# The first up pairs of an encoder layer: product 3 in a bank of its own, the order of their products, and the order of w_o's transposes

## The chip, the core and the metric

The kernel runs on one core of a Trainium2 chip, as one program. The time is that of the device in microseconds (us), the median of several executions. The engines are TensorE (PE, with PEld for its loads of weights, which run beside the matmuls), VectorE (DVE), ScalarE (ACT), GpSimd (POOL) and SyncE (SP). Each has its own instruction stream and works it off in order; they meet at semaphores. DMAs are issued by SP and POOL here. PSUM has eight banks of 128 partitions x 512 fp32 numbers; matmuls write there, and ScalarE and VectorE read from there.

## The reference

One layer of a streaming encoder on 512 tokens, in float32, cut to what matters (D_MODEL 2048, D_FF 5632, eight heads of 128):

```
h  = rms_norm(x, pre_mix_g)
z  = h @ w_in                        # [q | k | v | u]
m  = concat(chunked_attention(q, k, v, rel_bias),
            multiscale_pool(u, pool_w, pool_scale)) @ w_o
x  = x + rms_norm(m, post_mix_g)
h  = rms_norm(x, pre_ffn_g)
up = causal_dwconv(h @ w_up, conv_w, conv_b)      # 3 taps along the tokens
y  = (gelu(up[..., :D_FF]) * up[..., D_FF:]) @ w_down
x  = x + rms_norm(y, post_ffn_g)
```

The change lies where `h @ w_o` ends and `h @ w_up`, the convolution and the gate begin.

## The kernel before

**Numbers.** A float32 operand is split into a rounded part and the rest: `split(hi, lo, src)` is one ScalarE copy that rounds (line 140) and one VectorE subtraction (line 141). Names that end in h are rounded parts, names that end in l are rests. A product of two split operands needs three matmuls (`mm3`: hi by hi, hi by lo, lo by hi; lines 162 to 165).

**Seven products.** The large matrix products are made in blocks of two by two with seven block products instead of eight, numbered 1 to 7. For w_up this holds from the third *pair* on; a pair is 256 columns of w_up, and there are 44 pairs. The first two are *plain* (made with `mm3` into banks `up`, L162 to L165). The other 42 are counted by k from 0, and (k,i) is product i of pair k. Each such product multiplies a factor of h, which is made once, by a factor of w_up, which is made for each product, in `mm2`: eight matmuls of 128x512 (the rounded part of the weights, L170) and eight of 128x256 (the rests, L176). Products 6, 7 and 4 are *turned*: their narrow matmuls come first.

A product adds into a bank of PSUM, named q and a letter and k: products 1, 6, 7, 4 of a pair add up in bank a (qa_k), 5 and 3 in bank g (qg_k), and 2 has bank d (qd_k). Products 1, 5 and 2 begin a bank (`FIRST`); the others add onto what is there. As a bank also holds sums that are wanted in between, the function `keep(k, i)`, called right after the matmuls of (k,i), reads them out: after 1, one half is copied by ScalarE and the other added by VectorE to `first_parts`; after 2, VectorE adds both halves of qd there; after 5, ScalarE copies qg (L1413); after 6, ScalarE copies qa (L1418), and VectorE adds qg, which by then holds 5 and 3 (L1419); after 7, ScalarE copies qa (L1422), and VectorE adds the copy of 5; after 4, `keep_all(k)` puts the pair's four quarters together. So the next product that adds onto a bank must wait for the ScalarE copy of what stands there.

**Taps, gate, product.** A finished pair is convolved (`taps`: one ScalarE step L1309, two VectorE steps L1310 and L1311). Two pairs belong together: the first of them goes through gelu (`gate`, L1332), the second is multiplied by it on VectorE (`product`, L1342) in two halves, and the result goes to memory in two stores that POOL issues (L1345). The scratch tiles are four holders, m8, zc, x01 and x23, cut into parts: m8 holds the copy of 5, the sums of 6 and 7, and the value half before its multiplication, zc the finished pair and the gate.

**Weights' factors.** `Factors` makes the factor of each product, in the order of a list `order`. `load` issues the raw blocks on SP (wx or x, wy, wz). `make` splits a raw block into a tile pair (wfh, wfl) and, after products 1, 5, 6 and 3, has POOL add another block of w_up onto the same raw tile with an accumulating DMA (`add`, L1109): the block that is x for product 1 becomes the factor of 5, then 6, then 4, and y that of 3, then 7. Such a DMA must wait for the split before it, on ScalarE and VectorE, and the next split for the DMA. `get` is called ahead of each product: it counts the use and has the factors of up to AHEAD = 4 products made in advance (and up to 3 before `open` is set), and the raw loads run RAW - AHEAD = 6 further ahead. There are eight tiles for split weights (the ring w4), so four pairs hi and lo.

**What sets the order.** TensorE's instructions run in the order in which the program writes them. Those of all the other engines are put into an order by the compiler's scheduler, and where a ring or a pool hands out a tile, the writer waits for its last reader.

The list `order` begins with products 1 and 2 of the pairs 0 to 3, which run while the second half of h (tokens 256 to 511) is still being normalized, and among which `turn_back` transposes that half; then come the two plain pairs (the entries "w"), then (0,5), (0,3), and then all other products sorted by 7 k + place_of[i]. During the first plain pair `h_sums` makes the factors h5, h6 and h3 of h (tiles h50, h51, h60, h61, h30, h31). In that part gT0 to gT3 are the tiles of split h, made by the split at the end of `turn_back` (L141 with the output gT), and w00_0 to w00_3 and w10_0 to w10_3 the four weights of each plain pair.

`turn_back(0, pair, ...)` does the same for tokens 0 to 255, in eight steps of two blocks, called by `first_half(q)` behind the four pieces of the w_o product before (two steps for each piece). The steps 0 to 3 go to the tile a11, 4 to 7 to a12, and after each odd one a quarter is split.

Of the kernel before, what the change touches and what calls it, by code (L numbers as in the profile page):

```python
# [81 lines left out]
def encoder_layer(ctx: ExitStack, tc: tile.TileContext, x, xT, vecs, rel, post_mix, post_ffn,  # L82
# [7 lines left out]
    nc = tc.nc  # L90
# [15 lines left out]
    def bank(name):  # L106
        return psum.tile([P, 512], F32, tag="ps", name=name)
# [246 lines left out]
    hT = new_gT()  # L354
# [5 lines left out]
    for kb in range(KD):  # L360
        i, o = divmod(kb, 8)
# [9 lines left out]
        for what in "qk":  # L371
            _, hi, lo = first[f"{what}0_{i}"]
# [160 lines left out]
    BANK = {1: "a", 6: "a", 7: "a", 4: "a", 5: "g", 3: "g", 2: "d"}  # L533
    FIRST = 1, 5, 2
# [367 lines left out]
    if True:  # L902
# [104 lines left out]
        def turn_back(t0, pair, ps):  # L1007

            for k in range(2):
                kb = 2 * pair + k  # L1010
                for t in range(2):
                    nc.tensor.transpose(ps[:, k * T + t * P:k * T + (t + 1) * P],
                                        hn[t0 + t][:, kb * P:(kb + 1) * P], ident)
            v = wholes[pair // 4, t0 // 2]
            for k in range(2):
                kb = 2 * pair + k
                nc.scalar.activation(v[:, kb % 8, :], ps[:, k * T:(k + 1) * T], AF.Copy, scale=col(V_PREFFN, kb))
            if pair % 2:
                i = pair // 2 % 2
                split(*quarter(pair // 4, t0 // 2, i), v[:, 4 * i:4 * i + 4, :])  # L1020
# [8 lines left out]
        for t in range(2):  # L1029
            load_x(t, acc8(f"x{t}", "B"))  # L1030
        hT = new_gT()
        hT[1], hT[2] = hT[2], hT[1]
        x2(0, y11, 0, whole)
        x2(0, y12, 1, whole)
        keep_x(0)
# [21 lines left out]

        def first_half(q):
            for i in range(2):
                turn_back(0, 2 * q + i, wo_banks[4 + (2 * q + i) % 4])  # L1060

        finish_last(0, wo_product(4, 0, a22, first_half))
        load_x(3, h8(0, "x3"))
# [1 line left out]
        class Factors:  # L1065
# [3 lines left out]
            def __init__(self):  # L1069
                n = 2 * NU - PLAIN  # L1070

                self.alone, self.open = (1, 2, 3, n - 1), False
                place_of = {1: 0, 6: 8, 2: 2, 7: 10, 5: 4, 4: 12, 3: 6}
                begin = [(k, i) for k in range(4) for i in (1, 2)] + [(0, 5), (0, 3)]
                end = [(n - 1, 5), (n - 2, 6), (n - 1, 3), (n - 1, 1), (n - 2, 7), (n - 1, 6), (n - 2, 4),
                       (n - 1, 7), (n - 1, 2), (n - 1, 4)]
                order = sorted((7 * k + at, k, i) for k in range(n) for i, at in place_of.items())
                self.order = begin + [(k, i) for _, k, i in order if (k, i) not in begin + end] + end  # L1080
                self.order[8:8] = [("w", q) for q in range(4 * PLAIN)]
                self.raw, self.made, self.loaded, self.used = {}, [], 0, 0
# [58 lines left out]
            def get(self):  # L1141
                self.used += 1
                self.prefetch(0)
                self.prefetch(self.AHEAD if self.open else self.AHEAD - 1)
                v, self.made[self.used - 1] = self.made[self.used - 1], None
                return v

# [157 lines left out]
    if True:  # L1305
# [55 lines left out]
        def h_factor(i, kb):  # L1361
            if i in hs:
                return hs[i][kb // 4][:, kb % 4].rearrange("p a b -> p (a b)"), 0
            k, t = {1: (0, 0), 7: (0, 1), 2: (1, 0), 4: (1, 1)}[i]
            return hT[2 * k + kb // 4][:, kb % 4, 2 * t:2 * t + 2].rearrange("p a b -> p (a b)"), 1 - t
# [35 lines left out]
        def keep(k, i):  # L1401

            if i == 1:
                v = zs[k, "1"] = first_parts[:, k % 4, :]
                nc.scalar.activation(v, banks[k, "a"][:, :T], AF.Copy)
                nc.vector.tensor_add(v, banks[k, "a"][:, T:], v)
            elif i == 2:
                v, d = zs[k, "1"], banks.pop((k, "d"))
                nc.vector.tensor_add(v, d[:, :T], v)
                nc.vector.tensor_add(v, d[:, T:], v)  # L1410
            elif i == 5:
                zs[k, "5"] = raw_x("zb")[:, :S] if k == end else holder("m8")[1]
                nc.scalar.activation(zs[k, "5"], banks[k, "g"], AF.Copy)  # L1413
            elif i == 6:
                m = raw_x("zm") if k == end else holder("m8")[2]
                zs[k, "m"] = m.rearrange("p (a b c) -> p a b c", a=2, b=2)
                v = wide(zs[k, "m"][:, :1])
                nc.scalar.activation(v, banks[k, "a"], AF.Copy)  # L1418
                nc.vector.tensor_add(v, banks.pop((k, "g")), v)  # L1419
            elif i == 7:  # L1420
                v = wide(zs[k, "m"][:, 1:])
                nc.scalar.activation(v, banks[k, "a"], AF.Copy)  # L1422
                nc.vector.tensor_add(v, zs.pop((k, "5")), v)
            elif i == 4:
                keep_all(k)

# [12 lines left out]

        def seven(k, i):  # L1440
            w = factors.get()
            if i in FIRST:
                banks[k, BANK[i]] = bank(f"q{BANK[i]}_{k}")
            ps = banks[k, BANK[i]]
            mm2(ps, w, [h_factor(i, kb) for kb in range(8)], i in FIRST, i in TURNED)

        def first_left():

# [323 lines left out]
```

## Time and profile before

| what | us |
|---|---|
| median of three runs | 1864.54 (1862.0 to 1865.09) |
| the profiled execution's own time | 1864.22 |
| its span in the profile | 1862.4 |
| TensorE without work, start to 50 | 1.44 |
| 560 to 580, the first plain up pair begins | 1.58 |
| 620 to 700, the first of the 42 pairs | 5.10 |
| 1350 to 1440, the down projection begins | 2.59 |
| 1800 to the end | 8.2 |

The mean granted clock of TensorE over the span is 0.997 of full speed. The products (k,i) run from 620 to about 1370 us.

How the views are read: a timeline's row gives the start, the duration, the engine, the line of the program, the operation and its output and inputs (the buffers' numbers left out); a bracket at its end gives the time that the engine stood idle before the row and what ended it, with the line of the instruction that did. The table of waits has the waiting engine, output and line, the releaser behind the arrow, and then the sum in us, the number, and the longest. In the table by windows each engine has its busy time and, in parentheses, its count of instructions.

### The profile page before, as it was taken

The numbers are of one execution on the slowest core, as the hardware profiler recorded it, in microseconds if no ns is written. First come the engines' busy times: TensorE is split into PE (matmuls) and PEld (weight loads), VectorE is DVE, ScalarE is ACT, GpSimd is POOL, SyncE is SP. The second block draws the span as 40 slices with busy tenths as digits, with TensorE's granted clock in tenths as the row PEclk, the third lists the DMA queues.
The fourth block names the chain that finished last, engine by engine and source line by source line (L and its number), as shares of the span: only waits on it lengthen the run. The fifth ranks groups of instructions, "written<-read, shape, count | busy, mean of one in ns | idle before, by whom it ended". The sixth has DMA issues, their size and how long they took to land.

```text
span 1862.4 us, 25317 instructions
## 1 busy us (share of the span) xinstructions
PE 1843.5 (99%) x9514; PEld 1580.2 (85%) x9514; DVE 1482.2 (80%) x1772; ACT 1101.1 (59%) x1442; POOL 306.9 (16%) x407
## 2 busy tenths in 40 slices
PE   9999999999999999999999999999999999999998
PEld 7888888888888788888888888888888888888886
DVE  6988778888678677777787777877776899899876
ACT  7655455456586566665666656666555665565553
POOL 3412001100001212212122122221221001111101
PEclk9999999999999999999999999999999999999999
DMA  8599977999879888988988888888888977777785
GB/s 317 175 318 301 323 226 232 269 278 321 324 270 291 184 187 206 201 206 199 206 199 207 206 196 204 198 209 205 200 174 278 356 226 173 194 207 179 176 243 145
DMA packets 139546, 428.63 MB, mean 230 GB/s; under 512 B 12000, under 2 KB 15456, under 8 KB 133728
## 3 DMA queue, kind: packets, MB, share of 16 engines
q0 software_dynamic: 55440, 175.66, 47.0%
q1 hardware_dynamic: 83984, 251.36, 38.1%
q8 instruction: 75, 1.23, 0.3%
q14 instruction: 47, 0.39, 0.1%
HBM read 372.97 MB, written 104.33 MB: 256 GB/s over the span
## 4 chain that ended last, share of the span: by engine, by line
PE 66%; DMA 1%; DVE 1%; ACT 1%; issue 0%; POOL 0%; DVEq 0%; POOLq 0%; ACTq 0%
PE qa L170 16%; PE qa L176 8%; PE qg L170 8%; PE qg L176 4%; PE pa L165 4%; PE pa L162 4%; PE pa L164 4%; PE qd L170 4%; PE pg L165 2%; PE pg L162 2%; PE pg L164 2%; PE qd L176 2%; PE pd L164 1%; PE pd L165 1%; PE pd L162 1%; PE up L164 1%
## 5 line engine op out<-in xcount | busy, mean ns | idle before, releaser
L170 PE MATMUL qa<-gT,wfh 128*128 128x512 f32 x1176 | 295.9, 394 | 0.0
L141 DVE TENSOR_TENSOR wfl<-x,wfh 128x1024 fp32r<-128x1024 f32 x161 | 197.1, 1224 | 83.0 <-ACT wfh L140 76.8
L170 PEld LDWEIGHTS qa<-gT,wfh 128*128 128x128 f32 x1176 | 212.5, 190 | 38.2
L140 ACT ACTIVATE wfh<-x 128x1024 fp32r<-128x1024 f32 x161 | 170.1, 1056 | 88.9 <-PE qg L170 47.3
L1109 POOL DMA_DIRECT2D x<-in_w_up x122 | 104.7, 858 | 475.1 <-DVE wfl L141 435.7
L176 PE MATMUL qa<-gT,wfl 128*128 128x256 f32 x1176 | 165.1, 283 | 3.4 <-ACT m L1418 3.4
L170 PE MATMUL qg<-h,wfh 128*128 128x512 f32 x672 | 166.4, 390 | 1.9 <-ACT m L1413 1.9
L176 PEld LDWEIGHTS qa<-gT,wfl 128*128 128x128 f32 x1176 | 155.0, 192 | 8.8 <-ACT m L1418 4.7
L170 PEld LDWEIGHTS qg<-h,wfh 128*128 128x128 f32 x672 | 125.8, 188 | 28.9 <-ACT m L1413 2.9
L140 ACT ACTIVATE wfh<-wy 128x1024 fp32r<-128x1024 f32 x98 | 103.3, 1054 | 69.1 <-PE qd L170 49.3
L141 DVE TENSOR_TENSOR bl<-b,bh 128x2048 fp32r<-128x2048 f32 x56 | 127.1, 2286 | 18.6 <-ACT bh L140 11.7
L140 ACT ACTIVATE bh<-b 128x2048 fp32r<-128x2048 f32 x56 | 106.0, 1913 | 54.7 <-DVE b L1229 22.7
L141 DVE TENSOR_TENSOR wfl<-wy,wfh 128x1024 fp32r<-128x1024 f32 x98 | 119.4, 1218 | 16.9 <-ACT wfh L140 14.6
L162 PE MATMUL pa<-bh,ah 128*128 128x512 f32 x320 | 124.5, 389 | 0.0
L164 PE MATMUL pa<-bl,ah 128*128 128x512 f32 x320 | 124.5, 389 | 0.0
L165 PE MATMUL pa<-bh,al 128*128 128x512 f32 x320 | 124.5, 389 | 0.0
L176 PEld LDWEIGHTS qg<-h,wfl 128*128 128x128 f32 x672 | 91.7, 190 | 6.6
L170 PE MATMUL qd<-gT,wfh 128*128 128x512 f32 x392 | 97.0, 390 | 0.0
L176 PE MATMUL qg<-h,wfl 128*128 128x256 f32 x672 | 93.7, 282 | 0.0
L170 PEld LDWEIGHTS qd<-gT,wfh 128*128 128x128 f32 x392 | 73.2, 188 | 15.0
L170 PE MATMUL qa<-h,wfh 128*128 128x512 f32 x336 | 84.1, 392 | 0.0
L141 DVE TENSOR_TENSOR wfl<-wz,wfh 128x1024 fp32r<-128x1024 f32 x49 | 59.9, 1223 | 29.6 <-PE qa L170 26.8
(568 smaller groups left out, 4319.5 us busy)
## 6 DMA issues: line engine op xcount, KB each, us to landing
x<-in_w_up POOLq DMA_DIRECT2D x122, 512.0 KB, 5.9
b<-in_w_down SPq DMA_DIRECT2D x32, 1024.0 KB, 6.9
wt<-in_w_o POOLq DMA_DIRECT2D x24, 1024.0 KB, 14.9
wz<-in_w_up SPq DMA_DIRECT2D x42, 512.0 KB, 5.3
x<-in_w_up SPq DMA_DIRECT2D x42, 512.0 KB, 5.1
wy<-in_w_up SPq DMA_DIRECT2D x42, 512.0 KB, 4.0
wy<-in_w_up POOLq DMA_DIRECT2D x42, 512.0 KB, 6.1
sum<-part POOLq DMA_DIRECT2D x38, 512.0 KB, 6.7
```

The costliest lines, as they stand in the source:

```text
L140: rounded = nc.scalar.activation(hi, src, AF.Copy)
L141: rest = nc.vector.tensor_sub(lo, src, f32(hi))
L162: nc.tensor.matmul(ps, l[0], r[0], start=first, stop=False, skip_group_check=onto)
L164: nc.tensor.matmul(low, l[0], r[1], start=False, stop=False, skip_group_check=onto)
L165: nc.tensor.matmul(ps, l[1], r[0], start=False, stop=last, skip_group_check=onto)
L170: nc.tensor.matmul(ps, w[0][:, kb], pairs[kb][0], start=fresh and not kb, stop=last, skip_group_check=not fresh)
L176: nc.tensor.matmul(ps[:, sl], w[1][:, kb], pair[:, sl], start=False, stop=last, skip_group_check=not fresh)
L1109: nc.gpsimd.dma_start(self.raw[k, what], self.block(k, m, kh), accum_op=ALU.add)
```

## The change

It has three parts.

1. For k < 4, product 3 begins a bank of its own, e (qe_k), instead of adding onto qg after product 5. Nothing is copied out of a bank after 5 and after 3 any more for these four pairs; after 6, VectorE adds qg and then qe to the sum, and after 7 it adds qg, read from the bank, where it added the copy of 5. The products 5, 3, 6, 7, 4 of these pairs are put in another order, by 5 k + (0, 2, 4, 6, 8), so that products of two pairs alternate; from pair 4 on the order is as before, by 20 + 7 (k - 4) + place_of[i].
2. `get` has fewer factors made in advance before `open` is set: at most 9 less the number of those used.
3. `first_half` does the transposes of h's first 256 tokens in the order 0, 1, 4, 5, 2, 3, 6, 7, so that the first half of the second tile (a12) comes before the second half of the first, and the two tiles hT[1] and hT[2] are no longer exchanged.

```diff
--- before.py
+++ after.py
@@ -1029,7 +1029,6 @@
         for t in range(2):
             load_x(t, acc8(f"x{t}", "B"))
         hT = new_gT()
-        hT[1], hT[2] = hT[2], hT[1]
         x2(0, y11, 0, whole)
         x2(0, y12, 1, whole)
         keep_x(0)
@@ -1057,7 +1056,7 @@
 
         def first_half(q):
             for i in range(2):
-                turn_back(0, 2 * q + i, wo_banks[4 + (2 * q + i) % 4])
+                turn_back(0, (0, 1, 4, 5, 2, 3, 6, 7)[2 * q + i], wo_banks[4 + (2 * q + i) % 4])
 
         finish_last(0, wo_product(4, 0, a22, first_half))
         load_x(3, h8(0, "x3"))
@@ -1073,10 +1072,12 @@
 
                 self.alone, self.open = (1, 2, 3, n - 1), False
                 place_of = {1: 0, 6: 8, 2: 2, 7: 10, 5: 4, 4: 12, 3: 6}
-                begin = [(k, i) for k in range(4) for i in (1, 2)] + [(0, 5), (0, 3)]
+                begin = [(k, i) for k in range(4) for i in (1, 2)]
+                lone = {5: 0, 3: 2, 6: 4, 7: 6, 4: 8}
                 end = [(n - 1, 5), (n - 2, 6), (n - 1, 3), (n - 1, 1), (n - 2, 7), (n - 1, 6), (n - 2, 4),
                        (n - 1, 7), (n - 1, 2), (n - 1, 4)]
-                order = sorted((7 * k + at, k, i) for k in range(n) for i, at in place_of.items())
+                order = sorted([(5 * k + at, k, i) for k in range(4) for i, at in lone.items()] +
+                               [(20 + 7 * (k - 4) + at, k, i) for k in range(4, n) for i, at in place_of.items()])
                 self.order = begin + [(k, i) for _, k, i in order if (k, i) not in begin + end] + end
                 self.order[8:8] = [("w", q) for q in range(4 * PLAIN)]
                 self.raw, self.made, self.loaded, self.used = {}, [], 0, 0
@@ -1141,7 +1142,7 @@
             def get(self):
                 self.used += 1
                 self.prefetch(0)
-                self.prefetch(self.AHEAD if self.open else self.AHEAD - 1)
+                self.prefetch(self.AHEAD if self.open else min(self.AHEAD - 1, 9 - self.used))
                 v, self.made[self.used - 1] = self.made[self.used - 1], None
                 return v
 
@@ -1408,6 +1409,8 @@
                 v, d = zs[k, "1"], banks.pop((k, "d"))
                 nc.vector.tensor_add(v, d[:, :T], v)
                 nc.vector.tensor_add(v, d[:, T:], v)
+            elif i in (5, 3) and k < 4:
+                return
             elif i == 5:
                 zs[k, "5"] = raw_x("zb")[:, :S] if k == end else holder("m8")[1]
                 nc.scalar.activation(zs[k, "5"], banks[k, "g"], AF.Copy)
@@ -1416,11 +1419,13 @@
                 zs[k, "m"] = m.rearrange("p (a b c) -> p a b c", a=2, b=2)
                 v = wide(zs[k, "m"][:, :1])
                 nc.scalar.activation(v, banks[k, "a"], AF.Copy)
-                nc.vector.tensor_add(v, banks.pop((k, "g")), v)
+                nc.vector.tensor_add(v, banks[k, "g"] if k < 4 else banks.pop((k, "g")), v)
+                if k < 4:
+                    nc.vector.tensor_add(v, banks.pop((k, "e")), v)
             elif i == 7:
                 v = wide(zs[k, "m"][:, 1:])
                 nc.scalar.activation(v, banks[k, "a"], AF.Copy)
-                nc.vector.tensor_add(v, zs.pop((k, "5")), v)
+                nc.vector.tensor_add(v, banks.pop((k, "g")) if k < 4 else zs.pop((k, "5")), v)
             elif i == 4:
                 keep_all(k)
 
@@ -1439,10 +1444,11 @@
 
         def seven(k, i):
             w = factors.get()
-            if i in FIRST:
-                banks[k, BANK[i]] = bank(f"q{BANK[i]}_{k}")
-            ps = banks[k, BANK[i]]
-            mm2(ps, w, [h_factor(i, kb) for kb in range(8)], i in FIRST, i in TURNED)
+            at = "e" if i == 3 and k < 4 else BANK[i]
+            fresh = i in FIRST or at == "e"
+            if fresh:
+                banks[k, at] = bank(f"q{at}_{k}")
+            mm2(banks[k, at], w, [h_factor(i, kb) for kb in range(8)], fresh, i in TURNED)
 
         def first_left():
 
```

In the changed file the lines behind the first edits have higher numbers: the copy of 5 is L1416 there (1413 before), the copies after 6 and 7 L1421 and L1427 (1418 and 1422), the taps L1310 to L1312 (1309 to 1311), gelu L1333 (1332), the multiplication L1343 (1342). Three places show how the instructions move.

**The split of h that the first plain pair waits for.** These are rows of VectorE in the kernel before, shortly ahead of the first plain pair: w00_0l, w00_1l and w00_2l are rests of that pair's first three weights, gT0 is the first quarter of h's second half, and first_parts is what is kept of the products 1 and 2.

```order
L1406 TENSOR_TENSOR first_parts_5274<-qa_2_5371,first_parts_5274 128x256
L141 TENSOR_TENSOR w00_0l_5391<-w00_0r_5199,w00_0h_5390 128x1024
L1409 TENSOR_TENSOR first_parts_5274<-qd_2_5394,first_parts_5274 128x256
L141 TENSOR_TENSOR w00_1l_5414<-w00_1r_5217,w00_1h_5413 128x1024
L1410 TENSOR_TENSOR first_parts_5274<-qd_2_5394,first_parts_5274 128x256
L1406 TENSOR_TENSOR first_parts_5274<-qa_3_5417,first_parts_5274 128x256
L141 TENSOR_TENSOR w00_2l_5453<-w00_2r_5294,w00_2h_5452 128x1024
L141 TENSOR_TENSOR gT0_4822<-a21_5256,gT0_4822 128x4x256
```

In the changed kernel the same place reads:

```order
L1407 TENSOR_TENSOR first_parts_5274<-qa_2_5371,first_parts_5274 128x256
L141 TENSOR_TENSOR w00_0l_5391<-w00_0r_5199,w00_0h_5390 128x1024
L1410 TENSOR_TENSOR first_parts_5274<-qd_2_5394,first_parts_5274 128x256
L1407 TENSOR_TENSOR first_parts_5274<-qa_3_5413,first_parts_5274 128x256
L1411 TENSOR_TENSOR first_parts_5274<-qd_2_5394,first_parts_5274 128x256
L141 TENSOR_TENSOR w00_1l_5494<-w00_1r_5217,w00_1h_5493 128x1024
L141 TENSOR_TENSOR w00_2l_5498<-w00_2r_5294,w00_2h_5497 128x1024
L141 TENSOR_TENSOR gT0_4822<-a21_5256,gT0_4822 128x4x256
```

The rests w00_1l and w00_2l stand two rows and no row later than before; both are still ahead of gT0, behind the same four additions to first_parts.

**TensorE where the first four pairs end.** Rows of TensorE around the first product of pair 4 on bank g, a row for four matmuls that read alike; qg_4 is that bank, qa_3 bank a of pair 3, h50 to h31 are the factors of h for the products 5 and 3, and gT those for 7 and 4. Before:

```order
L170 MATMUL qg_4_6354<-h50_5655,wfh_6253 128x512 x4
L170 MATMUL qg_4_6354<-h51_5664,wfh_6253 128x512 x4
L176 MATMUL qg_4_6354<-h50_5655,wfl_6254 128x256 x4
L176 MATMUL qg_4_6354<-h51_5664,wfl_6254 128x256 x4
L176 MATMUL qa_3_5417<-gT1_4823,wfl_6278 128x256 x4
L176 MATMUL qa_3_5417<-gT3_4825,wfl_6278 128x256 x4
L170 MATMUL qa_3_5417<-gT1_4823,wfh_6277 128x512 x4
L170 MATMUL qa_3_5417<-gT3_4825,wfh_6277 128x512 x4
L170 MATMUL qg_4_6354<-h30_5674,wfh_6299 128x512 x4
L170 MATMUL qg_4_6354<-h31_5677,wfh_6299 128x512 x4
L176 MATMUL qg_4_6354<-h30_5674,wfl_6300 128x256 x4
L176 MATMUL qg_4_6354<-h31_5677,wfl_6300 128x256 x4
```

After:

```order
L176 MATMUL qa_3_5413<-gT2_4824,wfl_6257 128x256 x4
L176 MATMUL qa_3_5413<-gT3_4825,wfl_6257 128x256 x4
L170 MATMUL qa_3_5413<-gT2_4824,wfh_6256 128x512 x4
L170 MATMUL qa_3_5413<-gT3_4825,wfh_6256 128x512 x4
L170 MATMUL qg_4_6392<-h50_5657,wfh_6279 128x512 x4
L170 MATMUL qg_4_6392<-h51_5666,wfh_6279 128x512 x4
L176 MATMUL qg_4_6392<-h50_5657,wfl_6280 128x256 x4
L176 MATMUL qg_4_6392<-h51_5666,wfl_6280 128x256 x4
L170 MATMUL qg_4_6392<-h30_5676,wfh_6303 128x512 x4
L170 MATMUL qg_4_6392<-h31_5679,wfh_6303 128x512 x4
L176 MATMUL qg_4_6392<-h30_5676,wfl_6304 128x256 x4
L176 MATMUL qg_4_6392<-h31_5679,wfl_6304 128x256 x4
```

Before, product 4 of pair 3 (qa_3 from gT1 and gT3) stands between product 5 (h50, h51) and product 3 (h30, h31) of pair 4. In the changed kernel that product (qa_3 from gT2 and gT3 there, as hT[1] and hT[2] aren't exchanged) stands ahead of both, and the two products of pair 4 follow one another.

**ScalarE ahead of the copy that product (4,3) waits for.** Rows of ScalarE in the changed kernel that end in the copy of qg_4 (L1416); wfh_6303, wfh_6328, wfh_6353 and wfh_6388 are rounded weights of the products (4,3), (5,1), (4,6) and (5,2), L1406 the copy after (4,1), L1333 the gelu of a pair before and L1310 the tap that writes the value half into m8.

```order
L1406 ACTIVATE first_parts_5274<-qa_4_6284 128x256
L1333 ACTIVATE zc_5682<-zc_5682 128x1024
L140 ACTIVATE wfh_6303<-wy_6154 128x1024
L1427 ACTIVATE m8_5822<-qa_3_5413 128x512
L140 ACTIVATE wfh_6328<-x01_5587 128x1024
L140 ACTIVATE wfh_6353<-x23_5901 128x1024
L1437 ACTIVATE zc_5682<-qa_3_5413 128x256
L1310 ACTIVATE m8_5822<-zc_5682,vec_69 128x512
L140 ACTIVATE wfh_6388<-wz_6223 128x1024
L1416 ACTIVATE m8_5822<-qg_4_6392 128x512
```

The copy stands behind three roundings, the last copy from qa_3 and the tap. Before, the same copy (L1413 there) stood behind the copy after (3,7) and a rounding, ahead of the tap:

```order
L140 ACTIVATE wfh_6299<-wy_6151 128x1024
L140 ACTIVATE wfh_6325<-x01_5619 128x1024
L1422 ACTIVATE m8_5821<-qa_3_5417 128x512
L140 ACTIVATE wfh_6349<-x23_5923 128x1024
L1413 ACTIVATE m8_5821<-qg_4_6354 128x512
L140 ACTIVATE wfh_6372<-wz_6231 128x1024
L1432 ACTIVATE zc_5680<-qa_3_5417 128x256
L1309 ACTIVATE m8_5821<-zc_5680,vec_69 128x512
```

In the changed kernel VectorE's rows that belong to the same stretch are these; wfl_6280 is the rest of the weights of (4,5), and the two additions L1422 and L1424 are those of qg_3 and qe_3 after (3,6).

```order
L1311 SCALAR_TENSOR_TENSOR zc_5682<-zc_5682,vec_69 128x511
L141 TENSOR_TENSOR wfl_6257<-x23_5901,wfh_6256 128x1024
L1312 SCALAR_TENSOR_TENSOR zc_5682<-zc_5682,vec_69 128x510
L1311 SCALAR_TENSOR_TENSOR zc_5682<-zc_5682,vec_69 128x511
L1422 TENSOR_TENSOR m8_5822<-qg_3_6161,m8_5822 128x512
L1312 SCALAR_TENSOR_TENSOR zc_5682<-zc_5682,vec_69 128x510
L1424 TENSOR_TENSOR m8_5822<-qe_3_6206,m8_5822 128x512
L141 TENSOR_TENSOR wfl_6280<-x23_5901,wfh_6279 128x1024
L1407 TENSOR_TENSOR first_parts_5274<-qa_4_6284,first_parts_5274 128x256
L141 TENSOR_TENSOR wfl_6304<-wy_6154,wfh_6303 128x1024
```

The four tap steps (L1311, L1312) and the two additions stand ahead of the rest wfl_6280 of (4,5).

## The prediction

> **What bounds the kernel now.** I read the page first:
>
> ```profile
> span 1862.4 us, 25317 instructions
> ## 1 busy us (share of the span) xinstructions
> PE 1843.5 (99%) x9514; PEld 1580.2 (85%) x9514; DVE 1482.2 (80%) x1772; ACT 1101.1 (59%) x1442; POOL 306.9 (16%) x407
> ```
>
> TensorE is busy for 1843.5 of 1862.4 us. The change leaves the number and the kinds of its matmuls as they are, so it can only win or lose idle time of TensorE, of which there are 18.9 us, or clock. The table of TensorE's waits says which part of that lies where the change works:
>
> ```profile
> PE qa L176 <- ACT m L1418: 3.4, 3, 2.0
> PE qg L170 <- ACT m L1413: 1.9, 3, 0.9
> PE up L164 <- DVE gT L141: 1.6, 1, 1.6
> ```
>
> The first two are products that wait for ScalarE to copy the bank they want to add onto; the third is the first plain up pair, which waits for a split of h. The other idle time stands at the start, in the down projection and at the end. The timeline of TensorE shows each wait (bracket: idle time before the row, and what ended it):
>
> ```profile
> 619.96 1.98 PE L170 MATMUL qg<-h,wfh 128*128 128x512 f32 x8
> ...
> 623.70 2.11 PE L170 MATMUL qg<-h,wfh 128*128 128x512 f32 x8 [0.81 <-ACT m L1413]
> ...
> 630.25 1.21 PE L176 MATMUL qa<-gT,wfl 128*128 128x256 f32 x8 [0.69 <-ACT m L1418]
> ...
> 639.73 2.12 PE L170 MATMUL qg<-h,wfh 128*128 128x512 f32 x8 [0.86 <-ACT m L1413]
> ...
> 647.65 1.57 PE L176 MATMUL qa<-gT,wfl 128*128 128x256 f32 x8 [2.05 <-ACT m L1418]
> ...
> 652.11 2.01 PE L170 MATMUL qg<-h,wfh 128*128 128x512 f32 x8
> ...
> 654.91 1.12 PE L176 MATMUL qa<-gT,wfl 128*128 128x256 f32 x8
> ...
> 657.71 1.98 PE L170 MATMUL qg<-h,wfh 128*128 128x512 f32 x8
> ...
> 664.13 1.21 PE L176 MATMUL qa<-gT,wfl 128*128 128x256 f32 x8 [0.69 <-ACT m L1418]
> ```
>
> Here 0.81 + 0.69 + 0.86 + 2.05 + 0.69 = 5.10 us are lost among the first pairs. A product takes 2.80 us (652.11 to 654.91, 654.91 to 657.71), but the one from 647.65 to 652.11 takes 4.46, 1.66 more. The table by windows says why (columns: stretch, its length, busy PE, PEld, DVE, ACT and POOL with counts, granted clock, DMA):
>
> ```profile
> 560.00:580.00 20.00, 18.42 (x104) 15.74 (x103) 16.09 (x26) 12.89 (x23) 1.61 (x2) 1.00 0.86 276
> 648.00:650.00 2.00, 2.00 (x11) 1.81 (x10) 0.71 (x2) 0.74 (x1) 0.85 (x1) 0.57 0.83 274
> 650.00:652.00 2.00, 2.00 (x7) 1.56 (x6) 0.00 (x0) 0.31 (x1) 0.00 (x0) 0.58 0.93 119
> ```
>
> After the gap of 2.05 us the granted clock is 0.57 for some 3.4 us; after the 1.58 us at 573 it stayed 1.00. So the first pairs lose 5.10 + 1.66 = **6.76 us**, the whole prize of the reordering; the wait for h adds 1.58.
>
> **The waits that go.** Product 3 has a bank of its own for k < 4, so it waits for no copy of product 5 (0.81, 0.86). Product 7 no longer follows its own 6 directly: one other product of 2.80 us stands between, and so does one between 7 and 4. ScalarE's timeline says how much cover that needs:
>
> ```profile
> 638.13 1.06 ACT L140 ACTIVATE wfh<-wy 128x1024 fp32r<-128x1024 f32 x1 [4.14 <-DMA wy<-in_w_up]
> 639.10 0.58 ACT L1413 ACTIVATE m<-qg 128x512 f32<-128x512 f32 x1
> 639.58 0.80 ACT L1309 ACTIVATE zc<-zc,vec 128x512 f32<-128x512 f32 x1
> ...
> 646.07 1.04 ACT L1332 ACTIVATE zc<-zc 128x1024 f32<-128x1024 f32 x1
> 647.02 0.57 ACT L1418 ACTIVATE m<-qa 128x512 f32<-128x512 f32 x1
> ```
>
> The copy itself is 0.58; the rest of a wait is the queue ahead of it (a rounding that waits for an accumulating load, a gelu). One rounding and the copy, 1.06 + 0.58, fit in 2.80. The accumulating loads that a factor needs between its roundings also get about four products, 11.2 us, instead of two. The four copies of 5 on ScalarE (0.58 each) become four more adds on VectorE. All five waits and the half clock behind them go: -6.76.
>
> **The wait that comes.** The order rows show product (4,3) directly behind (4,5). Pair 4 isn't one of the first four: its 3 adds onto bank g, after copy L1416 of 5. That copy stands on ScalarE behind the rounding for (4,6), a tap (L1310) and another rounding. (4,6)'s weights are an accumulating load, which POOL issues only when VectorE has done the split wfl_6280 of (4,5). So I follow that chain with these rows (VectorE's and POOL's timelines; durations start to start where rows follow directly: a split 1.14, an add 0.60, a tap step 0.77):
>
> ```profile
> 628.99 0.68 DVE L1342 TENSOR_TENSOR zc<-zc,m 128x512 f32<-128x512 f32 x1
> ...
> 659.11 0.42 DVE L1433 TENSOR_TENSOR zc<-qa,zc 128x256 f32<-128x256 f32 x1
> ...
> 663.60 1.22 DVE L141 TENSOR_TENSOR wfl<-wy,wfh 128x1024 fp32r<-128x1024 f32 x1
> 664.74 0.68 DVE L1419 TENSOR_TENSOR m<-qg,m 128x512 f32<-128x512 f32 x1
> 665.34 0.74 DVE L1310 SCALAR_TENSOR_TENSOR m<-zc,vec,m 128x511 f32<-128x511 f32 x1
> 666.11 0.75 DVE L1311 SCALAR_TENSOR_TENSOR m<-zc,vec,m 128x510 f32<-128x510 f32 x1
> ```
> ```profile
> 629.97 1.52 POOL L1345 DMA_DIRECT2D gd<-zc  x2 [3.89 <-DVE zc L1342]
> ```
>
> A store is issued 0.30 after its product is done (628.99 + 0.68 to 629.97), the second 0.76 later. The landings, issue to arrival: the DMA view of 625 to 690 us, then all adds (L1109) and all stores (L1345) from 600 to 1370 us:
>
> ```profile
> x<-in_w_up POOLq DMA_DIRECT2D x9, 512.0 KB, 5.6
> ...
> gd<-zc POOLq DMA_DIRECT2D x4, 256.0 KB, 3.8
> ```
> ```profile
> DMA to landing us min/median/max: 5.2/5.9/8.8
> ```
> ```profile
> DMA to landing us min/median/max: 3.1/4.7/6.0
> ```
>
> I take the medians of the stretch itself, 5.6 and 3.8, and keep the others for the range. Without a stall, product n of the new order (n = 0 is (0,5) at 619.96) starts at 619.96 + 2.80 n: (2,6), n = 12, ends at 656.4, and (4,3), n = 23, could start at **684.4**. From 656.4 VectorE's queue holds, up to the last multiplication of the second value half, three splits, four tap steps and five adds: 3.42 + 3.08 + 3.00 = 9.5, so 665.9. The second store: + 0.30 + 0.76 + 3.8 = 670.8. Only then may ScalarE's tap L1310 overwrite the stored tile: + 0.80 = 671.6. VectorE's rows from that tap to wfl_6280 are four tap steps, a split, two adds and the split itself: 3.08 + 1.14 + 1.20 + 1.22 = 6.6, so 678.2. The load for (4,6): + 0.30 + 5.6 = 684.1. Then the rounding 1.06, its split 1.14, the add before the tap 0.42, the tap 0.80, the next rounding 1.06 and the copy 0.58: 689.2. TensorE so waits 689.2 - 684.4 = **4.8 us**, more than twice the gap that halved the clock, so 1.66 comes on top: 6.46. An earlier stall of a few tenths, as at (3,7), whose copy waits for the same store, would come off the 4.8, since the chain's end stays where it is. With the fastest landings (5.2, 3.1) the wait is 3.7, with the slowest (8.8, 6.0) 10.2.
>
> **The other edits cost and bring nothing.** "Fewer weights ahead of h's splits" isn't what VectorE gets: the order rows show w00_1l and w00_2l still ahead of gT0, in a queue without a gap:
>
> ```profile
> 572.31 1.21 DVE L141 TENSOR_TENSOR w_2l<-w_2r,w_2h 128x1024 fp32r<-128x1024 f32 x1
> 573.45 1.21 DVE L141 TENSOR_TENSOR gT<-a,gT 128x1024 fp32r<-128x1024 f32 x1
> ```
> ```profile
> 574.71 0.50 PE L164 MATMUL up<-gT,w_0h 128*128 128x512 f32 x1 [1.58 <-DVE gT L141]
> ```
>
> The same instructions stand before that split, so it ends at 574.66 again and the 1.58 stays; bounds are a full loss of the wait (-1.58) and one more split (+1.14), and I take 0, as the rows say. The reordered transposes write the tile a12 with the second of w_o's four pieces instead of the third; its slot was freed by the stores of x (SyncE's timeline, the DMA view of 505 to 530 us, and ScalarE's copy of the second piece):
>
> ```profile
> 510.87 1.53 SPq L992 DMA_DIRECT2D out<-x  x2
> ```
> ```profile
> out<-x SPq DMA_DIRECT2D x2, 1024.0 KB, 5.0
> ```
> ```profile
> 532.56 1.55 ACT L1017 ACTIVATE a<-m,vec 128x256 f32<-128x256 f32 x4
> ```
>
> The stores landed some 5.0 after their issue, by about 517.4, and the copy runs at 532.56, so no wait arises; swapping the two tiles of h only renames them. One load of SP's queue (the second x01) moves ahead of w10_1r, a weight of the second plain pair, which runs only when all of the first plain pair's products are through. Each of these at 0.
>
> **Sum.** -6.76 + 6.46 = -0.3 us. The profiled execution took 1864.22 (span 1862.4 and 1.8 around it), 0.3 below the median 1864.54 of three runs, which reach from 1862.0 to 1865.1. So 1864.5 - 0.3 = **1864.2**.
>
> **The rivals.**
> 1. The new wait doesn't form, or is short: the chain would have to end 4.8 us sooner. For it: it is a queue on two engines, whose order I know but whose landings vary. Against it: the fastest landings take only 1.1 off. Then the full 6.76 goes: 1857.8. Chance 0.13.
> 2. The new wait is long (the case on the slower side). If the two stores and the load land as slowly as the slowest rows, the wait is 10.2, and with 1.66 the loss is 11.9 against 6.76: 1869.6. It is slower by over 0.2% (3.7 us) from a wait of 8.8 on. Both must be slow at once. Chance 0.05.
> 3. The wait forms, but the clock isn't halved, as after the 1.58 us: 1864.2 - 1.7 = 1862.5. Here the rows give one gap of 2.05 with and one of 1.58 without. Chance 0.12.
> The Trainium skill, "TensorE: Matmul & The Clock Gate", section "Part 1: The HAM clock gate", has a rule that speaks for rival 3: the clock falls to half only after at least one wholly idle window of about 3.4 us, and windows run free. This trace doesn't agree: 2.05 us of idleness brought a clock of 0.57. By that rule a wait of 4.8 us halves the clock in only some starts (an estimate from the page: 1.4 of 3.4 phases), and the sum would be about a microsecond lower.
>
> **Numbers.** The forecast, with a wait of 3.7 to 8.8 and the half clock, has 0.70; the rivals 0.13, 0.05 and 0.12. About 0.2% (3.7 us) is what a measurement of this kernel can tell from no change. Faster by more than that is rival 1: 0.13; slower rival 2: 0.05; the same the rest, 0.82. The range takes in the forecast (1863.1 at a wait of 3.7, up to 1867 at some 7.5), rival 3, and runs that scatter by 1.5 us: 1860.5 to 1867.0.
>
> **What would show it.** In the changed profile: no wait of TensorE for copies between 620 and 673 us; one wait of 3.7 to 8.8 us near 684, ended by ScalarE's copy of qg at L1416, at product (4,3); a granted clock near 0.57 for some 3.4 us behind it; the wait of 1.6 us of up L164 unchanged at 573. Wrong would be: no wait there (rival 1), a wait elsewhere that repeats after each k, or the wait for h gone.

## The result and the profile after

| kernel | us, median (range) | runs | against before, 95% interval |
|---|---|---|---|
| before | 1864.88 (1861.25 to 1866.95) | 20 | |
| changed | 1867.26 (1864.49 to 1872.83) | 20 | 1.0017 (1.001 to 1.0024) |

The changed kernel is slower by 2.4 us. That is inside what I called the same (0.2%, 3.7 us), but 0.3 us above the upper end of the range, and on the other side of the forecast of -0.3 us. The profiled execution is the quickest of the twenty (1864.49, span 1862.6), and its mean granted clock, 0.998, is the highest of them; the others have 0.994 to 0.997. So the median has to be read beside it: by this clock, a usual execution of this kernel ran longer at the halved clock than the profile shows.

TensorE's waits in the changed kernel (columns as before: sum, number, longest):

```profile
PE qg L170 <- ACT m L1416: 5.5, 1, 5.5
PE qa L176 <- ACT m L1421: 2.1, 1, 2.1
PE up L164 <- DVE gT L141: 1.6, 1, 1.6
```

The five short waits among the first pairs have become two long ones; the wait for h is the same 1.6 us. Its timeline shows where they stand (bracket: idle time, and what ended it):

```profile
620.26 1.98 PE L170 MATMUL qg<-h,wfh 128*128 128x512 f32 x8
...
672.22 1.11 PE L176 MATMUL qa<-gT,wfl 128*128 128x256 f32 x8
675.46 1.21 PE L176 MATMUL qa<-gT,wfl 128*128 128x256 f32 x8 [2.13 <-ACT m L1421]
...
678.35 1.98 PE L170 MATMUL qd<-gT,wfh 128*128 128x512 f32 x8
...
684.25 1.98 PE L170 MATMUL qg<-h,wfh 128*128 128x512 f32 x8
...
692.71 3.41 PE L170 MATMUL qg<-h,wfh 128*128 128x512 f32 x8 [5.54 <-ACT m L1416]
...
696.91 2.00 PE L170 MATMUL qa<-gT,wfh 128*128 128x512 f32 x8
```

From 620.26 to the end of (4,1), at 673, nothing waits. Then (3,7) waits 2.13 and (4,3) 5.54, and (4,3) takes 696.91 - 692.71 = 4.20 instead of 2.80, so 1.40 more at the halved clock, which the table by windows shows (the clock third from the end):

```profile
692.00:694.00 2.00, 1.29 (x3) 1.09 (x4) 1.97 (x4) 1.08 (x3) 0.00 (x0) 0.53 0.95 143
694.00:696.00 2.00, 2.00 (x7) 1.52 (x7) 1.12 (x2) 0.81 (x1) 0.00 (x0) 0.61 0.87 223
```

In all 2.13 + 5.54 + 1.40 = **9.07 us**, where the kernel before lost 6.76 in its profile: 2.3 us more. The medians differ by 2.4. That the two agree so well is in part luck, as the profile is of the quickest execution and as the clock isn't halved behind the same gap in every execution (see the run with only the other two parts).

The two profiled executions differ by 0.3 us only. One cause stands far from the change, where the down projection begins (table by windows, the clock third from the end; before, then changed):

```profile
1440.00:1442.00 2.00, 2.00 (x7) 1.59 (x6) 2.00 (x1) 2.00 (x3) 0.00 (x0) 0.54 1.00 420
1442.00:1444.00 2.00, 2.00 (x7) 1.59 (x6) 1.09 (x1) 0.45 (x1) 0.00 (x0) 0.60 0.33 70
```
```profile
1440.00:1442.00 2.00, 1.27 (x6) 1.06 (x7) 0.49 (x1) 2.00 (x3) 0.00 (x0) 1.00 1.02 426
1442.00:1444.00 2.00, 2.00 (x10) 1.66 (x9) 1.80 (x1) 2.00 (x2) 0.00 (x0) 1.00 0.91 381
```

Here the clock was halved in the execution of before and not in this one, which hides about 1.7 us of the loss; the remaining 0.3 us or so is not assigned.

### The profile page after: what moved, and what is told of

It reads as the page before. It is cut to its first block, busy times and chain, and to the rows that moved or that the text cites. A ratio compares the mean times of both kernels' runs of the same rounds, so it can differ in the third digit from the quotient of the medians.

```text
span 1862.6 us, 25315 instructions
## 1 busy us (share of the span) xinstructions
PE 1840.5 (99%) x9514; PEld 1579.1 (85%) x9514; DVE 1484.1 (80%) x1776; ACT 1100.1 (59%) x1438; POOL 306.8 (16%) x407
## 4 chain that ended last, share of the span: by engine, by line
PE 65%; DMA 2%; issue 1%; DVE 1%; ACT 0%; POOL 0%; POOLq 0%; DVEq 0%; ACTq 0%
PE qa L170 15%; PE qa L176 8%; PE qg L170 8%; PE qg L176 4%; PE pa L162 4%; PE pa L164 4%; PE pa L165 4%; PE qd L170 4%; PE pg L162 2%; PE pg L164 2%; PE pg L165 2%; PE qd L176 2%; DMA bl<-rw02l 1%; PE pd L164 1%; PE pd L165 1%
## 5 line engine op out<-in xcount | busy, mean ns | idle before, releaser
L170 PE MATMUL qg<-h,wfh 128*128 128x512 f32 x640 | 159.5, 392 | 5.5 <-ACT m L1416 5.5
L170 PEld LDWEIGHTS qg<-h,wfh 128*128 128x128 f32 x640 | 121.0, 189 | 30.9 <-ACT m L1416 5.7
L176 PEld LDWEIGHTS qg<-h,wfl 128*128 128x128 f32 x640 | 87.3, 190 | 6.2
L176 PE MATMUL qg<-h,wfl 128*128 128x256 f32 x640 | 89.2, 282 | 0.0
```

Of the source, the lines that this page charges most:

```text
L170: nc.tensor.matmul(ps, w[0][:, kb], pairs[kb][0], start=fresh and not kb, stop=last, skip_group_check=not fresh)
L176: nc.tensor.matmul(ps[:, sl], w[1][:, kb], pair[:, sl], start=False, stop=last, skip_group_check=not fresh)
```

## The experiments

Nine kernels ran, each timed beside the kernel before on the same chip. The ratio is estimated from all executions, so it need not be the quotient of the two medians; where its interval holds 1, the runs can't tell the kernel from the one before.

| kernel | us, median | runs | before | ratio (95% interval) |
|---|---|---|---|---|
| only the up products | 1869.64 | 6 | 1864.59 | 1.0027 (1.0015 to 1.004) |
| only the other two parts | 1864.01 | 11 | 1864.59 | 0.9999 (0.999 to 1.0008) |
| own bank, order of before | 1863.73 | 11 | 1864.29 | 0.9999 (0.999 to 1.0007) |
| product stored from m8 | 1860.35 | 11 | 1864.59 | 0.998 (0.997 to 0.999) |
| stores on SyncE's queue | 1865.22 | 10 | 1864.29 | 1.0009 (1.0 to 1.0018) |
| own bank for pair 4 too | 1865.54 | 11 | 1864.59 | 1.0002 (0.9993 to 1.0011) |
| (5,1) ahead of (4,3) | 1863.3 | 12 | 1864.68 | 0.9991 (0.9982 to 0.9999) |
| from m8, bank for pair 4 | 1856.38 | 5 | 1864.29 | 0.9963 (0.9949 to 0.9976) |
| from m8, (5,1) ahead | 1856.01 | 5 | 1864.29 | 0.9956 (0.9943 to 0.9968) |

**Which part of the change.** First the up products alone:

```diff
-turn_back(0, (0, 1, 4, 5, 2, 3, 6, 7)[2 * q + i], ...)
+turn_back(0, 2 * q + i, ...)
+hT[1], hT[2] = hT[2], hT[1]
-self.prefetch(self.AHEAD if self.open else min(self.AHEAD - 1, 9 - self.used))
+self.prefetch(self.AHEAD if self.open else self.AHEAD - 1)
```

> Only the first part of the change: product 3's own bank and the new order of the first four up pairs; the weights ahead of h's splits and w_o's transposes as before. Theory A (the loss comes from the new order: stores of the gated product land late, a tap on ScalarE waits for them, and the products (3,7) and (4,3) wait behind it): as the changed kernel, 1867 us (1866 to 1868.5), with a wait of some 2 us at (3,7), one of 4.5 to 6.5 us at (4,3), half the clock behind it. Theory B (the loss comes from the reordered transposes or from the weights): 1862 us or less, without most of these waits.

The loss is all there, in a median 1.1 us above the range of theory A. Its timeline has the same two waits, here with the clock halved behind both:

```profile
676.50 1.46 PE L176 MATMUL qa<-gT,wfl 128*128 128x256 f32 x8 [3.23 <-ACT m L1422]
677.77 3.36 PE L170 MATMUL qa<-gT,wfh 128*128 128x512 f32 x8
680.97 2.00 PE L170 MATMUL qd<-gT,wfh 128*128 128x512 f32 x8
...
693.72 3.26 PE L170 MATMUL qg<-h,wfh 128*128 128x512 f32 x8 [4.23 <-ACT m L1417]
```

The opposite, the other two parts without the up products (the same lines put into the kernel before):

> Only the second and third part: fewer weights ahead of h's splits, w_o's transposes reordered; the up products as before. Theory A: as the kernel before, 1864.9 us (1864 to 1866), with the five waits of 5.1 us among the first up pairs and the 1.6 us wait of the first plain up pair. Theory B: 2 to 5 us slower than before.

No difference, as theory A has it, and the old waits are all there, with one more of 0.81 us at (2,3); theory B falls. One thing is missing in its profile, though: the half clock behind the long wait of (1,7). The gap is the same as before, 2.06 us, but the matmuls behind it keep their full speed:

```profile
649.86 1.22 PE L176 MATMUL qa<-gT,wfl 128*128 128x256 f32 x8 [2.06 <-ACT m L1417]
650.92 2.00 PE L170 MATMUL qa<-gT,wfh 128*128 128x512 f32 x8
```

So the 1.66 us of half clock that the prediction counts as lost before are not lost in every execution.

The up products alone were some 2 us slower than the whole change; the two intervals overlap. In the two profiles it is mostly the clock that differs: it is halved behind (3,7) as well in the one of the up products alone, which takes 1.7 us, and for nearly 7 us at the down projection, and in neither place in the one of the changed kernel.

**What the bank does without the order.**

```diff
-order = sorted([(5 * k + at, k, i) ... lone ...] + [(20 + 7 * (k - 4) + at, k, i) ...])
+order = sorted((7 * k + at, k, i) for k in range(n) for i, at in place_of.items())
```

> The changed kernel with product 3's own bank for the first four pairs, but their products in the order of before (7 k + place). It tells what the bank does without the order. Expected: the two or three waits of product 3 (0.8 us each) go, those of product 7 behind its own 6 (0.7, 2.05, 0.7 us, with half the clock behind the long one) stay, no new wait at (4,3), since (3,4) stands between it and (4,5); 1864.6 - 1.7 = 1862.9 us (1861.5 to 1864.5). If the own bank alone is what brings the new wait: 1866 us or more.

The time can't be told from that of before, but nor from 1.7 us less, which lies just inside the interval (-1.9 to +1.3 us); the profile tells more. The waits of product 3 did go, the two of 0.69 us at (0,7) and (2,7) stay, and the wait of (1,7) took over what was gained:

```profile
648.17 1.32 PE L176 MATMUL qa<-gT,wfl 128*128 128x256 f32 x8 [4.12 <-ACT m L1420]
```
```profile
646.57 1.06 ACT L1332 ACTIVATE zc<-zc 128x1024 f32<-128x1024 f32 x1 [0.88 <-DVE zc L1311]
647.54 0.58 ACT L1420 ACTIVATE m<-qa 128x512 f32<-128x512 f32 x1
```

Before, the copy for (1,7) ran from 647.02 to 647.59; here it runs from 647.54 to 648.12. TensorE came 1.6 us sooner and found the copy no sooner: 4.12 instead of 2.05. The copy's time is set on ScalarE, behind a gelu, not by TensorE. The three waits sum to 5.50 us, no less than the 5.10 before. The same thing happens at (4,3) in the changed kernel.

**What the copy of qg_4 waits for.** ScalarE in the changed kernel, then the landing of the two stores in 660 to 680 us (shortest, median, longest):

```profile
668.76 1.07 ACT L140 ACTIVATE wfh<-x 128x1024 fp32r<-128x1024 f32 x1 [0.57 <-PE qa L176]
673.41 1.52 ACT L1310 ACTIVATE zc<-zc,vec 128x512 f32<-128x512 f32 x2 [3.58 <-DMA gd<-zc]
674.83 0.58 ACT L1421 ACTIVATE m<-qa 128x512 f32<-128x512 f32 x1
...
687.74 1.06 ACT L140 ACTIVATE wfh<-x 128x1024 fp32r<-128x1024 f32 x1 [5.48 <-DMA x<-in_w_up]
...
690.42 0.81 ACT L1310 ACTIVATE m<-zc,vec 128x512 f32<-128x512 f32 x1 [1.35 <-DVE zc L1438]
691.14 1.04 ACT L140 ACTIVATE wfh<-wz 128x1024 fp32r<-128x1024 f32 x1
692.09 0.58 ACT L1416 ACTIVATE m<-qg 128x512 f32<-128x512 f32 x1
```
```profile
DMA to landing us min/median/max: 5.7/6.1/6.5
```

ScalarE stands still for 3.58 us until the stores have landed, and the copy that (3,7) needs (L1421) is the next in its queue. Later it stands 5.48 us for the load of (4,6), with the copy for (4,3) behind. To take the stores out, the gated product of pairs 0 and 1 is written to m8's first two parts and stored from there (shortened):

```diff
+if u == 1: c = m8[:, :1024] viewed as two parts, part j
-nc.vector.tensor_mul(g[:, j, :], g[:, j, :], c)
+nc.vector.tensor_mul(c if u == 1 else g[:, j, :], g[:, j, :], c)
+if u == 1: g = both parts of m8
```

> The changed kernel, but the second gated product (pairs 0 and 1) is written into the value half's own scratch (m8, whose second part is unused for the first four pairs) and stored from there, so the tap that begins the next gate has no store to wait for. Theory A: the wait at (3,7) goes, and of the 5.5 us at (4,3) 0.4 to 1.0 us stays (the copy of product 5 stands behind a tap that must follow product (3,4), and behind a rounding); no half clock; 1867.3 - 8.4 = 1858.9 us (1857.5 to 1860.5). Rival C (the accumulating loads on POOL's queue are themselves too slow for the new order, the stores only stand beside them): a wait of 3 us or more stays at (4,3) with half the clock behind it, 1862 to 1865 us.

The wait at (3,7) went, and the kernel is faster than before. But at (4,3) 2.42 us stayed, with half the clock:

```profile
687.40 3.18 PE L170 MATMUL qg<-h,wfh 128*128 128x512 f32 x8 [2.42 <-ACT m L1423]
```

The load for (4,5) is late there. POOL issued it behind the stores and right after another; the DMA view of these two issues (7.6 is the median of the two; the first alone has 5.9, so the second took some 9.3), and ScalarE's rounding that waits for it:

```profile
x<-in_w_up POOLq DMA_DIRECT2D x2, 512.0 KB, 7.6
```
```profile
673.82 1.06 ACT L140 ACTIVATE wfh<-x 128x1024 fp32r<-128x1024 f32 x1 [2.10 <-DMA x<-in_w_up]
```

So A has the larger part, and C a part too. The median of 1860.35 lies within the range of A, 1.5 above its number, but not by A's account: A had at most 1.0 us of wait at (4,3) and no half clock, and here (4,3) waits 2.42 and then takes 4.45 us instead of 2.80.

The edit also did more than take the stores out of the chain. As the value half has scratch of its own, VectorE finished the second multiplication 4.2 us sooner (at 661.59 instead of 665.78), and POOL issued the stores at 661.90, ahead of the two accumulating loads. There they landed in 2.7 us, by about 665.3, before ScalarE's tap ran at 665.54 in this kernel. So this run does not tell which of the two took the wait away: that the stores no longer hold the gate's buffer, or that they go out sooner. That the tap waits for the stores in the changed kernel is shown by its own row, 3.58 us.

**Is it the queue or the engines?**

```diff
-nc.gpsimd.dma_start(gd[...], g[...])
+(nc.sync if u == 1 else nc.gpsimd).dma_start(gd[...], g[...])
```

> The changed kernel, but the two stores of the second gated product go out on SyncE's queue instead of POOL's; all else and the order of every engine's own work as in the changed kernel. Theory A (the stores land 6.1 us after issue because two accumulating loads of 512 KB stand right ahead of them on the same queue): they land in 3 to 4 us, ScalarE's tap starts some 2.5 us sooner, the wait at (3,7) is nearly gone (under 0.6 us), 2 to 4 us stay at (4,3), in all 1862 to 1865 us. Rival D (the DMA engines are shared, whatever the queue): the stores take 5.5 to 6.5 us again, the waits stay at 2 and 5.5 us, 1866 to 1869 us.

From SyncE's queue, on which nothing had been issued since 658.94, the stores took 6.0 to 6.2 us:

```profile
DMA to landing us min/median/max: 6.0/6.1/6.2
```

Theory A's reason for the late stores is wrong, and D has the landing right; neither has the time (1865.22 lies 0.2 above A's range and 0.8 below D's). The windows of the changed kernel fit D (second from the end: the mean busy share of the 16 DMA engines):

```profile
662.00:664.00 2.00, 2.00 (x11) 1.65 (x11) 2.00 (x4) 0.79 (x2) 0.85 (x1) 1.00 0.07 10
664.00:666.00 2.00, 2.00 (x18) 1.96 (x17) 2.00 (x4) 1.09 (x2) 0.86 (x1) 1.00 1.02 139
666.00:668.00 2.00, 2.00 (x12) 1.70 (x11) 1.65 (x3) 1.23 (x2) 1.50 (x2) 1.00 1.02 195
668.00:670.00 2.00, 2.00 (x14) 1.74 (x13) 1.43 (x2) 1.26 (x2) 0.00 (x0) 1.00 1.06 236
670.00:672.00 2.00, 2.00 (x11) 1.65 (x10) 0.00 (x0) 0.00 (x0) 0.00 (x0) 1.00 1.00 387
```

Next to nothing moves at 662 to 664; then two accumulating loads (issued at 662.41 and 664.21), the two stores (666.08 and 666.84) and two raw loads of SyncE run at once, and the engines are full for eight microseconds. The Trainium skill says this in "DMA: Bandwidth & Descriptors", section "Issuing engines are not separate DMA queues": transfers started by different engines end up on the same 16 DMA engines and interleave there. This run agrees: 6.1 us from either queue. The landing also goes with the order of issue: in the five profiles in which the stores follow them (the changed kernel, the up products alone, SyncE's queue, and the two runs of the next part), they land in 5.7 to 7.6 us; in the three in which they are stored from m8 and go out ahead of them, in 2.5 to 2.8.

The waits were smaller than in the profile of the changed kernel all the same, 1.05 at (3,7) and 4.85 at (4,3): SyncE issues the two stores in 0.95 us where POOL takes 1.50, so ScalarE's tap starts at 672.67 instead of 673.41, and the load for (4,6) then lands in 6.2 us instead of 6.9. These 1.8 us less of waiting are about what the time fell by, some 1.5 us, each kernel taken against its own run of before.

**The neighbours (4,5) and (4,3).** First a bank of its own for product 3 of pair 4 too (each `k < 4` of the change becomes `k < 5`, the order stays):

> The changed kernel, but pair 4 too has product 3 in its own bank, so (4,3) needs no copy of product 5. Theory A: the 5.5 us at (4,3) and the half clock behind it go, the 2.1 us at (3,7) stay (ScalarE's queue waits for the stores there), and half the clock may follow these: 1867.3 - 7 = 1860.4 us (1859 to 1863). Rival C: the late weights of (4,6) hold up (4,6) instead, a wait of 2 us or more there, 1863 to 1866 us.

The median is 1865.54, not 1860.4. (4,3) no longer waits, but (3,7) waits 2.80 with the clock halved, and there is a new wait further on:

```profile
678.89 1.88 PE L176 MATMUL qa<-gT,wfl 128*128 128x256 f32 x8 [2.80 <-ACT m L1421]
680.58 2.93 PE L170 MATMUL qa<-gT,wfh 128*128 128x512 f32 x8
...
713.36 2.12 PE L170 MATMUL qg<-h,wfh 128*128 128x512 f32 x8 [1.99 <-ACT m L1416]
```
```profile
711.07 1.06 ACT L140 ACTIVATE wfh<-x 128x1024 fp32r<-128x1024 f32 x1 [4.63 <-DMA x<-in_w_up]
712.03 0.80 ACT L1310 ACTIVATE zc<-zc,vec 128x512 f32<-128x512 f32 x1
712.74 0.57 ACT L1416 ACTIVATE m<-qg 128x512 f32<-128x512 f32 x1
```

That is (5,3), behind the copy of product 5 of pair 5, which stands behind a rounding that waited 4.63 us for its load. Rival C's kind of wait, though not at (4,6) where I had put it.

Then (5,1) exchanged with (4,3) in the changed kernel:

```diff
+order = [{(4, 3): (25, 5, 1), (5, 1): (24, 4, 3)}.get(o[1:], o) for o in order]
```

> The changed kernel with (5,1) ahead of (4,3) and nothing else: the stores of the gated product stay as they are. Theory A (the end of the chain from the stores over the tap, the split of (4,5), the load for (4,6) and its rounding to the copy of qg_4 stays where it is, and TensorE waits for it whatever stands between): the 2.1 to 3.2 us at (3,7) stay, the 5.5 us at (4,3) shrink by the 2.8 us of the product put between, to 2 to 3 us, half the clock behind one of them; 1867.3 - 2.8 = 1864.5 us (1863 to 1866). If the neighbourhood of (4,5) and (4,3) is the whole cause: no wait at (4,3), 1861 us or less.

As theory A has it, and a microsecond better than its number:

```profile
676.83 1.21 PE L176 MATMUL qa<-gT,wfl 128*128 128x256 f32 x8 [2.76 <-ACT m L1422]
677.88 3.42 PE L170 MATMUL qa<-gT,wfh 128*128 128x512 f32 x8
...
693.63 2.12 PE L170 MATMUL qg<-h,wfh 128*128 128x512 f32 x8 [1.02 <-ACT m L1417]
```

(3,7) waits 2.76 us with the clock halved, and the 5.5 us at (4,3) have shrunk to 1.02. What stands between two neighbours is taken off the wait, and so is what TensorE loses ahead of it; the chain isn't shortened (its copy of qg_4 ends at 693.58, at 692.67 in the changed kernel).

**Both together.** The product stored from m8 and pair 4's own bank:

> Both mends: the second gated product is stored from m8's scratch, and pair 4 has product 3 in its own bank. Theory A: no wait at (3,7) nor (4,3), no half clock there, 1858 us (1857 to 1859.5). Theory C (the accumulating loads are late when they follow one another closely, and the wait shows at the next copy that stands behind a rounding): a wait of some 2 us at (5,3), behind the copy of product 5 of pair 5, as the run with pair 4's own bank alone showed, 1860 to 1862 us.

The product stored from m8 and (5,1) ahead of (4,3):

> The second gated product is stored from m8's scratch, and (5,1) is made ahead of (4,3), so one product of 2.8 us stands between (4,5) and (4,3) again, as at every later pair boundary but this. The run without this exchange kept 2.4 us at (4,3), less than 2.8. Theory A and C: no wait at (4,3) or under 0.5 us, no half clock, 1858.3 us (1857 to 1860). If the exchange only moves the wait (the next copy of a product 5 behind a late rounding): 1.5 us or more at (5,3), 1860 to 1862 us.

Both are faster than any other version, and beat both kernels, with medians below the ranges that they were given (by 0.6 and 1.0 us). In the first, theory C's wait at (5,3) is 0.39 us, not 2. The second is 8.3 us below before. Its only wait for a copy anywhere in the up products is this:

```profile
PE qg L170 <- ACT m L1424: 0.2, 1, 0.2
```

Of the first pairs' 6.76 us nearly all are gained, at 0.16 us of loss. The rest of the 8.3 isn't settled by one profile: its span is 1852.5, and no half clock follows the waits at the down projection in it.

## Why the prediction was wrong

**The prize was right, but for its clock.** All five waits and the half clock behind them are gone from the profile, 6.76 us, and nothing waits for a copy from 620 to 673. The waits stand in both profiles of the old first pairs (5.10 us before, 5.94 with only the other two parts), the 1.66 us of half clock in the first alone. Where the new wait was taken away as well, the kernel came out at 1856.01, 8.3 us below before; the prediction gave 6.76 us to that case (1857.8), so some 1.5 us of this gain were not in it.

**The other edits were right**, at nothing. They alone give 0.9999, and the wait for h is 1.56 us in the changed profile, as the rows of VectorE's order said.

**The place and the chain of the new wait were right**: at (4,3), ended by the copy of qg_4 at L1416, with half the clock behind. **Its size was wrong**: 4.8 us for the sum of the waits at (3,7) and (4,3), where 2.13 + 5.54 = 7.67 came. The working, step by step:

| end of | predicted | measured |
|---|---|---|
| second multiplication of the value half | 665.9 | 665.78 |
| second store landed | 670.8 | 673.3 |
| the split wfl_6280 | 678.2 | 680.46 |
| the load for (4,6) landed | 684.1 | 687.7 |
| the copy of qg_4 | 689.2 | 692.67 |

The third row is from VectorE's timeline, the load's landing from the DMA view of its one issue at 680.76:

```profile
679.24 1.22 DVE L141 TENSOR_TENSOR wfl<-x,wfh 128x1024 fp32r<-128x1024 f32 x1
```
```profile
x<-in_w_up POOLq DMA_DIRECT2D x1, 512.0 KB, 6.9
```

The step that failed is "I take the medians of the stretch itself, 5.6 and 3.8": the store took 6.5 instead of 3.8 and the load 6.9 instead of 5.6, which makes 4.0 us, of which 0.5 came back on ScalarE and VectorE. Without its waits TensorE would have come to (4,3) at 685.04, 0.6 later than the 684.4 of the prediction, so the wait is 2.9 us longer than predicted. VectorE's and ScalarE's parts of the chain were right to within half a microsecond.

In most of the stretch from which I took the landings, POOL issued its accumulating loads 5 to 6 us apart (five of them from 643.38 to 665.11), and two of the stores 2.8 us behind the last. Where transfers came closer there, right behind these stores, the loads issued at 669.38 and 671.65 took 6.8 and 7.6 us; the median hides them. In the changed kernel two loads and the two stores go out within 4.5 us (662.41 to 666.84), and later three loads within 3.7 us (680.76 to 684.44). The medians of before hold for the traffic of before. Whether it was TensorE's pauses that had kept the transfers apart is not shown.

The store came out slower than the slowest of before (6.0), the load between the median and the slowest (8.8). The condition of rival 2, "both must be slow at once", was no coincidence to be given 0.05: in all five profiles in which the stores follow the two loads, the second store takes 6.0 to 7.6 us and the load for (4,6) 6.2 to 6.9. With the measured wait the sum is 9.07 - 6.76 = +2.3 us, for the +2.4 measured.

The range was too narrow: its upper end held a wait of 7.5 us, although the forecast itself went up to 8.8, and the measured waits sum to 7.67. Another 0.4 us is no fault of the chain: the kernel before came out at 1864.88, not at the 1864.5 from which the sum starts. The executions reach 1872.83.

**An earlier wait** at (3,7) did come off the one at (4,3), as the prediction had it: the end of the chain decides, 692.67, whichever product TensorE waits in. The run with the old order and the own bank shows the same in the order of before: waits that were taken off its front came back at (1,7).

**Rival 3**, that the clock isn't halved behind the new wait, was wrong for (4,3): it was halved in each of the three profiles with a wait of over 4 us there (the changed kernel, the up products alone, the stores on SyncE's queue).

## What to carry to other kernels

Removing an engine's waits pays only if what ends the next wait moves too: follow that chain over all engines and DMAs to its end, and reckon with TensorE arriving earlier at an unmoved end. Here the waits went for good only when the store that held the gate's buffer was taken out of the chain, which also sent it out sooner, and the two products that share a bank were separated as well, by another product between them or by a bank of their own. And when a change brings transfers close together, price them by a stretch where they run close together, not by the median of a stretch in which they come one by one.

## What the runs showed of the hardware

The clock is halved behind gaps of two to three microseconds, and not by their length alone: it was halved behind the gaps of 2.42, 2.76, 2.80 and 3.23 us above, and not behind the one of 2.13; before, it was behind the one of 2.05 at (1,7), and in the run with only the other two parts it was not behind the same gap of 2.06. Two short gaps close together can do it too. At the down projection, first the up products alone (timeline, then the window behind the gaps), then the changed kernel:

```profile
1440.74 0.50 PE L162 MATMUL pd<-bh,ah 128*128 128x512 f32 x1 [1.15 <-ACT ah L140]
1442.60 0.80 PE L164 MATMUL pd<-bl,ah 128*128 128x512 f32 x1 [1.36 <-DMA bl<-rw02l]
```
```profile
1442.00:1446.00 4.00, 3.40 (x8) 2.73 (x9) 2.29 (x1) 4.00 (x4) 0.00 (x0) 0.50 0.93 388
```
```profile
1438.76 0.49 PE L162 MATMUL pd<-bh,ah 128*128 128x512 f32 x1 [1.15 <-ACT ah L140]
1440.72 0.50 PE L164 MATMUL pd<-bl,ah 128*128 128x512 f32 x1 [1.48 <-DMA bl<-rw02l]
```

The clock is 0.50 behind 1.15 and 1.36 us in the one, until about 1448.5, and stays 1.00 behind 1.15 and 1.48 in the other. The Trainium skill, "TensorE: Matmul & The Clock Gate", section "Part 1: The HAM clock gate", has free-running windows of some 3.4 us, which fits that the same gaps end differently, but it asks for a wholly idle window, and none of the gaps named here was that long.
